# Both parts of split weights written by GpSimd's DMAs, in a two-layer decoder trunk

## The chip, the core and the metric

The kernel runs on one core of one Trainium2 chip. The metric is device time in microseconds of one execution: 842.21 us before the change, the median of 3 runs (840.75 to 844.86). The core has five engines that work side by side, each through its own queue of instructions: TensorE (PE; the loading of its weights is listed as PEld), VectorE (DVE), ScalarE (ACT), GpSimd (POOL) and SyncE (SP, which here only issues DMAs). DMAs are carried out by 16 transfer engines that all queues share.

## The reference, cut to what matters

Two layers over 520 rows: a prompt of 512 positions and 8 sample rows. Layer 0 is one wide input projection (1024 to 7 x 1024), a convolution of width 31 with a layer norm (A), a short gated convolution (B), and an output projection; layer 1 projects to u, v and a gate (3 x 2048), mixes v within chunks of 128 positions, and projects back. After each comes a layer norm of the residual sum.

```
z = einsum('bld,de->ble', x, w_in)                         # layer 0: a_val, a_gate, b_post, c_pre, h, g
a = silu(layer_norm(causal_dwconv(a_val * sigmoid(a_gate))))
bo = b_post * causal_dwconv(c_pre * h)
x = layer_norm(alpha * x + einsum('ble,ed->bld', concat(a, bo) * silu(g), w_out))
...
u, v, g = split(einsum('bld,de->ble', x, w_in_c))          # layer 1
y = gelu(u) * (tril(w_s) @ layer_norm(gelu(v)) + b_s) * silu(g)
x = layer_norm(alpha * x + einsum('ble,ed->bld', y, w_out_c))
```

Everything is float32.

## The kernel before

The channels lie on the 128 partitions, the 520 rows along the free dimension. All projection weights are cut into 136 **units**, each a tile of 128 x 1024 float32 (512 KB): 1024 input channels as 8 k tiles of 128, by 128 output channels. One unit gives 128 output channels for all rows.

TensorE multiplies in float32r, which keeps fewer bits than float32. So every operand is split into two float32r parts: hi, the value cast to float32r, and lo, the value less hi. A product is hi·hi + lo·hi + hi·lo, three matmuls for each k tile and half of the rows (`mm2`, L152 to L163): 8 x 2 x 3 = 48 matmuls of 260 columns per unit. Both parts of a unit are needed from its second matmul on.

The first two units come with the input rows and are split in pieces (L177 to L213). The other 134 go through `load_unit` (L116): SyncE issues the load into a raw tile (L119; three buffers), ScalarE casts it to hi (L121), and VectorE or GpSimd subtracts hi from raw to give lo (L124). GpSimd has units 4 to 45 and 66 to 83 (`ON_POOL`, L127), VectorE the rest. The hi and lo tiles come from 12 buffers (`W`), six units' worth; units 70, 71, 134 and 135 (`EXTRA`) lie in another pool. `unit(n)` (L132) hands out unit n and loads ahead to unit n + 5 (`LEAD`). So the tiles of unit n can be written once TensorE has finished unit n - 6.

The order of the instructions of each engine is set by a scheduler when the kernel is built, from the order of the code, priorities (`background` for the wide convolution, `soon` for some steps) and what each instruction waits for. On the chip each engine then follows that order strictly: an instruction that waits holds back all that stand behind it.

The stages in order of TensorE's work: units 0 to 31, in turns of gate, val, c and h (L283 to L339), while VectorE runs the wide convolution (`acc`, L269, 240 steps) and the short one (`sB`, L332, 16 steps); post (L388), gb (L406) and the first half of the output projection (`z_o`, L453); ga; the second half of the projection with the layer norm (`out_part`, L473); then layer 1: v (L622 to L643, units 72 to 87), u and gc with the mix (`c_group`, L728), the first half of the output projection (`z_q`), u and gc again, and `out_part` for the end. `out_part` goes through its eight units twice, once for each half of the rows, and ends with the norm.

On GpSimd there are, besides its subtractions, small copies of the 8 sample rows (L307, L326, L612, L725), the stores of the convolution caches, two loads (L588, L590) and some steps of the last layer norm (L537, L549).

Of the kernel before, what the change touches and what calls it, by code (L numbers as in the profile page):

```python
# [9 lines left out]
F32 = mybir.dt.float32  # L10
# [3 lines left out]
ALU = mybir.AluOpType  # L14
AX = mybir.AxisListType

P = 128
D = 1024
# [5 lines left out]
KT = 8  # L24
# [8 lines left out]

# columns of the packed per-channel parameters
PA_W = 0
# [15 lines left out]
def decoder_kernel(  # L51
# [19 lines left out]
    nc = tc.nc  # L71
# [3 lines left out]
    wpool = ctx.enter_context(tc.tile_pool(name="wpool", bufs=1))  # L75
# [35 lines left out]

# [1 line left out]
    n_units = 2 + wu.shape[0]  # L113
    units = [None, None]

    def load_unit(wtag=("W", 12)):  # L116
        n = len(units)
        raw = wpool.tile([P, KT, P], F32, tag="raw", name=f"raw_{n}", bufs=3)
        nc.sync.dma_start(raw, wu[n - 2])  # L119
        hi = wpool.tile([P, KT, P], F32R, tag=wtag[0], name=f"whi_{n}", bufs=wtag[1])  # L120
        nc.scalar.copy(hi, raw)  # L121
        lo = wpool.tile([P, KT, P], F32R, tag=wtag[0], name=f"wlo_{n}", bufs=wtag[1])
        eng = nc.gpsimd if n in ON_POOL else nc.vector
        eng.tensor_tensor(lo, raw, hi.bitcast(F32), op=ALU.subtract)  # L124
        units.append((hi, lo))

    ON_POOL = set(range(4, 46)) | set(range(66, 84))  # L127
    EXTRA = set()
# [35 lines left out]

    # products of a constant until the first rows are there, so that the array's clock is up by then
    warm = const.tile([P, P], BF16, name="warm")
# [4 lines left out]

    # the input rows come with the first two weight units, one k tile after the other, and the
    # products follow in that order
    xh, xl = [], []
# [4 lines left out]
    for k in range(KT):  # L179
# [7 lines left out]
        cuts = 2 if k == 0 else 1  # L187
# [29 lines left out]
    nc.sync.dma_start(pa, pa_in)  # L217
    # powers of two, so float32r holds them as well
    ones_r = const.tile([P, P], F32R, name="ones_r")
# [10 lines left out]

    # ================= layer 0 =================
    unit(1)
# [49 lines left out]
    n = 0  # L282
    for i in range(KT):  # L283
# [56 lines left out]

    # the sample rows of both convolutions
    nc.gpsimd.dma_start(cbs_out, xb)
# [5 lines left out]
        op=ALU.mult,  # L348
# [21 lines left out]

    # layer norm of the wide convolution over the channels, then silu
    def mean_of(m, src, name):
        """the sum of src / D over the channels, from its two float32r parts"""
        both = tpool.tile([P, T], F32R, tag="B", name=f"parts_{name}", bufs=4)
        nn = src.shape[-1]
        hi, lo = both[:, :nn], both[:, TH : TH + nn]
        nc.scalar.copy(hi, src)
        nc.vector.tensor_tensor(lo, src, hi.bitcast(F32), op=ALU.subtract)
        nc.tensor.matmul(m, ones_r, hi, start=True, stop=False)
        nc.tensor.matmul(m, ones_r, lo, start=False, stop=True)  # L380
# [13 lines left out]
    def split_y(i, g, other, tag, parts):  # L394
        """y = g * other as its two parts, in that many cuts of the rows"""
        h = y_slot(F32R, f"yh_{tag}{i}")
        lo = y_slot(F32R, f"yl_{tag}{i}")
        for j in range(parts):
            c = slice(j * T // parts, (j + 1) * T // parts)
            nc.vector.tensor_tensor(g[:, c], g[:, c], other[:, c], op=ALU.mult)  # L400
            nc.scalar.copy(h[:, c], g[:, c])
            nc.vector.tensor_tensor(lo[:, c], g[:, c], h[:, c].bitcast(F32), op=ALU.subtract)
        yh.append(h)
        yl.append(lo)
# [68 lines left out]
    def out_part(base, c0, c1, yh, yl, res, lnc, done, last=False, pool_sub=()):  # L473
        """The second half of an output projection for the rows c0..c1, the residual, and the layer
        norm over the channels. The sums of the norm are of the rows less the mean of their first
        512 channels, so that no large mean cancels in the variance."""
        c = slice(c0, c1)
# [107 lines left out]

    # ================= layer 1 =================
    wt = wpool.tile([P, NH, P], F32, tag="M", name="wt", bufs=4)
    nc.gpsimd.dma_start(wt, wsT_in)  # L588
    bs = wpool.tile([P, NH, P], F32, tag="M", name="bs", bufs=4)
    nc.gpsimd.dma_start(bs, bs_in)  # L590
    # wt[s, h, t] is kept where s <= t
    nc.gpsimd.affine_select(
        wt, wt, pattern=[[0, NH], [1, P]], compare_op=ALU.is_ge, fill=0.0, base=0, channel_multiplier=-1
    )
    # and its float32r parts, for the column sums
    wth, wtl = [], []
# [53 lines left out]
    def v_finish():  # L650
# [5 lines left out]
        for i in range(NV):  # L656
            for c in range(NC):
# [7 lines left out]
                )  # L665
        # column sums of the causal weights, for the shift of the norm
        for j in range(2):
# [5 lines left out]
            )  # L673
        # the sample rows' layer norm
        ssum = tiny.tile([P, NS], F32, name="ssum")
# [113 lines left out]
def _units(w, e0, e1):  # L789
    """[1024, e] columns e0..e1 as [n, 128 (k inside), 8 (k tile), 128]"""  # L790
    w = w[:, e0:e1]
    n = (e1 - e0) // P
    return w.reshape(KT, P, n, P).transpose(2, 1, 0, 3)


def _chan(a, n):
    """[..., n*128] -> [128, n, ...]"""
    a = a.reshape(a.shape[:-1] + (n, P))
    k = a.ndim
    return a.transpose((k - 1, k - 2) + tuple(range(k - 2)))  # L800
# [86 lines left out]
```

## Time and profile before

| | |
|---|---|
| Median of 3 runs | 842.21 us (840.75 to 844.86) |
| Span of the profiled execution, first to last instruction | 840.8 us |
| TensorE's granted clock, mean | 0.991 |
| ScalarE's casts L121 | 134, 1047 ns each |
| GpSimd's subtractions L124 | 60, 2434 ns each |
| VectorE's subtractions L124 | 74, 1222 ns each |
| Wide convolution L269 on VectorE | 240, 748 ns each |

The page of the profile gives no other time of its own execution than the span. In the rows that follow, a group of instructions reads: line, engine, operation, output<-inputs, shapes, count, then busy time in us and the mean of one in ns, then the idle time of the engine just before them and what ended it. Rows of DMA issues read: output<-input, issuing queue, count, KB each, median us from issue to landing. A row of waits reads: who waited <- whom for, us in total, times, the longest. In the chain of waits and the timeline a row starts with its start and its length in us. In a tile's own view the durations are the shortest, the median and the longest in ns.

The busy shares of the engines in 40 equal slices of the span (digits are tenths; 9 is 90% or more):

```
PE   9989999998999999999999999999999999999994
DVE  5899999999994487356696333495455433625566
ACT  5423322333124346333466533333432133333243
POOL 0844355544340000024252711101000000000022
DMA  8533333223223452424050522204223233222011
```

### The profile page before, as it was taken

How to read it: one execution, taken by the hardware profiler on the slowest of the kernel's cores; microseconds unless marked ns; L12 is line 12 of the kernel's file. 1: busy time of each engine (PE TensorE's matmuls, PEld its weight loads, DVE VectorE, ACT ScalarE, POOL GpSimd, SP SyncE). 2: the span in 40 equal slices, each digit the busy share in tenths (PEclk: the TensorE clock that was granted, in tenths of full speed). 3: DMA queues.
4: the chain of work that ended last, by engine and by line, in shares of the span. 5: the costliest groups of instructions: out<-in, count | busy, mean ns of one | idle time of the engine just before them, and what ended most of it. 6: DMA issues, size and time to landing. Idle time of an engine off the chain costs nothing.

```text
span 840.8 us, 15982 instructions
## 1 busy us (share of the span) xinstructions
PE 816.4 (97%) x6792; PEld 813.8 (97%) x6792; DVE 557.8 (66%) x894; ACT 309.5 (37%) x470; POOL 193.7 (23%) x178
## 2 busy tenths in 40 slices
PE   9989999998999999999999999999999999999994
PEld 8989999998999999999999999999999999999993
DVE  5899999999994487356696333495455433625566
ACT  5423322333124346333466533333432133333243
POOL 0844355544340000024252711101000000000022
PEclk9999999999999999999999999999999999999998
DMA  8533333223223452424050522204223233222011
GB/s 301 164 103 101 101 103 102 96 82 130 72 79 101 122 166 66 126 76 126 26 166 12 171 81 82 95 24 156 77 76 95 82 101 94 83 79 99 1 51 51
DMA packets 27110, 82.38 MB, mean 98 GB/s; under 512 B 3568, under 2 KB 7296, under 8 KB 27040
## 3 DMA queue, kind: packets, MB, share of 16 engines
q1 hardware_dynamic: 26000, 79.01, 30.1%
q0 software_dynamic: 1040, 2.36, 0.7%
q8 instruction: 53, 0.87, 0.4%
q14 instruction: 17, 0.14, 0.1%
HBM read 77.91 MB, written 3.44 MB: 97 GB/s over the span
## 4 chain that ended last, share of the span: by engine, by line
PE 71%; DVE 23%; DMA 2%; issue 2%; ACT 1%; SPq 0%; POOL 0%; ACTq 0%; DVEq 0%; POOLq 0%
DVE acc L269 14%; PE z_gc L157 11%; PE z_u L157 11%; PE z_p L141 9%; PE z_v L157 7%; PE z_q L157 5%; PE z_o L157 5%; PE z_gb L157 5%; PE z_ga L157 5%; PE z_post L157 4%; PE z_v L141 4%; DVE sB L332 3%; DMA raw<-in_wu 2%; PE mix L713 2%; PE vt L615 1%
## 5 line engine op out<-in xcount | busy, mean ns | idle before, releaser
L121 ACT CAST whi<-raw 128x1024 fp32r<-128x1024 f32 x134 | 140.0, 1047 | 300.6 <-issue 66.6
L124 POOL TENSOR_TENSOR wlo<-raw,whi 128x1024 fp32r<-128x1024 f32 x60 | 145.6, 2434 | 262.6 <-ACT whi L121 262.3
L124 DVE TENSOR_TENSOR wlo<-raw,whi 128x1024 fp32r<-128x1024 f32 x74 | 90.2, 1222 | 131.0 <-ACT whi L121 131.0
L269 DVE SCALAR_TENSOR_TENSOR acc<-apad,pa,acc 128x512 f32<-128x512 f32 x240 | 166.6, 748 | 2.5 <-ACT acc L266 0.8
L157 PE MATMUL z_gc<-x1h,whi 128*128 128x260 f32 x256 | 72.9, 285 | 0.0
L157 PE MATMUL z_u<-x1h,whi 128*128 128x260 f32 x256 | 72.4, 283 | 0.0
L157 PE MATMUL z_gc<-x1h,wlo 128*128 128x260 f32 x256 | 72.0, 281 | 0.0
L157 PE MATMUL z_u<-x1l,whi 128*128 128x260 f32 x256 | 72.0, 281 | 0.0
L157 PE MATMUL z_gc<-x1l,whi 128*128 128x260 f32 x256 | 72.0, 281 | 0.0
L157 PE MATMUL z_u<-x1h,wlo 128*128 128x260 f32 x256 | 72.0, 281 | 0.0
L157 PEld LDWEIGHTS z_u<-x1h,wlo 128*128 128x128 f32 x256 | 48.1, 188 | 0.1
L157 PEld LDWEIGHTS z_gc<-x1h,wlo 128*128 128x128 f32 x256 | 48.2, 188 | 0.0
L157 PEld LDWEIGHTS z_u<-x1h,whi 128*128 128x128 f32 x256 | 48.1, 188 | 0.1
L157 PEld LDWEIGHTS z_gc<-x1l,whi 128*128 128x128 f32 x256 | 48.1, 188 | 0.0
L157 PEld LDWEIGHTS z_u<-x1l,whi 128*128 128x128 f32 x256 | 48.1, 188 | 0.0
L157 PEld LDWEIGHTS z_gc<-x1h,whi 128*128 128x128 f32 x256 | 48.1, 188 | 0.0
L725 POOL COPY mix<-mixs 128x8 f32<-128x8 f32 x16 | 3.5, 226 | 186.5 <-DVE gu L752 174.1
L157 PE MATMUL z_v<-x1h,whi 128*128 128x260 f32 x160 | 46.0, 287 | 0.0
L157 PE MATMUL z_v<-x1h,wlo 128*128 128x260 f32 x160 | 45.0, 281 | 0.0
L157 PE MATMUL z_v<-x1l,whi 128*128 128x260 f32 x160 | 44.9, 281 | 0.0
L157 PE MATMUL z_post<-xh,whi 128*128 128x260 f32 x128 | 36.8, 288 | 4.2 <-DVE sB L392 4.2
L157 PE MATMUL z_h<-xh,whi 128*128 128x260 f32 x128 | 36.9, 288 | 4.0 <-DVE apad L306 4.0
(259 smaller groups left out, 2758.5 us busy)
## 6 DMA issues: line engine op xcount, KB each, us to landing
raw<-in_wu SPq DMA_DIRECT2D x134, 512.0 KB, 3.6
xr<-in_xT SPq DMA_DIRECT2D x8, 260.0 KB, 4.6
x<-in_xT SPq DMA_DIRECT2D x7, 260.0 KB, 4.4
out_y<-r SPq DMA_DIRECT2D x8, 130.0 KB, 1.8
out_y<-out SPq DMA_DIRECT2D x4, 260.0 KB, 2.2
raw_s<-in_w SPq DMA_DIRECT2D x8, 128.0 KB, 4.2
xs<-in_cache_a SPq DMA_DIRECT2D x2, 496.0 KB, 9.2
out_cas<-xs POOLq DMA_DIRECT2D x2, 496.0 KB, 4.5
```

The costliest lines, as they stand in the source:

```text
L121: nc.scalar.copy(hi, raw)
L124: eng.tensor_tensor(lo, raw, hi.bitcast(F32), op=ALU.subtract)
L141: nc.tensor.matmul(ps, a[:, k, :], b[k][:, c], start=(k == 0 and j == 0), stop=(k == KT - 1 and j == 2),)
L157: nc.tensor.matmul(z[h][:, :TH], a[:, k, :], b[k][:, hs(h)], start=(k == 0 and j == 0), stop=(k == KT - 1 and j == 2),)
L269: nc.vector.scalar_tensor_tensor(acc[i], apads[i][:, j : j + SEQ], pa[:, i, PA_W + j : PA_W + j + 1], acc[i], op0=ALU.mult, op1=ALU.add,)
L332: nc.vector.scalar_tensor_tensor(s[:, :SEQ], ch[:, j : j + SEQ], pa[:, i, PB_W + j : PB_W + j + 1], s[:, :SEQ], op0=ALU.mult, op1=ALU.add,)
L615: nc.tensor.transpose(m[:, c * P : (c + 1) * P], vt[i][:, c * P : (c + 1) * P], ident)
L713: nc.tensor.matmul(m[:, c * P : (c + 1) * P], vtok[i][:, c * P : (c + 1) * P], wt[:, h, :], start=True, stop=True)
L725: nc.gpsimd.tensor_copy(t[:, SEQ:], mixs[:, i, :])
```

## The change

The raw tile goes, and with it the choice between VectorE and GpSimd. GpSimd issues a DMA that reads the weights as float32 and writes them as float32r into hi, casting on the way. ScalarE writes -hi into lo. GpSimd then issues a second DMA that reads the same weights again and adds them to lo in place, so that lo holds the weights less hi. Each unit is so read twice from memory, and the low part crosses ScalarE before its second DMA may start. The units, their buffers, the lead and all else stay as they were.

```diff
     def load_unit(wtag=("W", 12)):
         n = len(units)
-        raw = wpool.tile([P, KT, P], F32, tag="raw", name=f"raw_{n}", bufs=3)
-        nc.sync.dma_start(raw, wu[n - 2])
         hi = wpool.tile([P, KT, P], F32R, tag=wtag[0], name=f"whi_{n}", bufs=wtag[1])
-        nc.scalar.copy(hi, raw)
+        nc.gpsimd.dma_start(hi, wu[n - 2])
         lo = wpool.tile([P, KT, P], F32R, tag=wtag[0], name=f"wlo_{n}", bufs=wtag[1])
-        eng = nc.gpsimd if n in ON_POOL else nc.vector
-        eng.tensor_tensor(lo, raw, hi.bitcast(F32), op=ALU.subtract)
+
+        nc.scalar.mul(lo, hi.bitcast(F32), -1.0)
+        nc.gpsimd.dma_start(lo, wu[n - 2], accum_op=ALU.add)
         units.append((hi, lo))
 
-    ON_POOL = set(range(4, 46)) | set(range(66, 84))
     EXTRA = set()
```

The rest of the diff takes comments out. Lines of the changed kernel stand two lower than before: the DMAs are L119 and L123, the negation is L122.

The scheduler orders GpSimd's queue anew. Three places show how. In the rows a name is followed by the unit's number (or that of another tile) and a buffer number: `whi_86_5688` is the high part of unit 86.

GpSimd at the start of layer 0, behind its first memsets, before the change (it waits for the first gate tile, then subtracts for units 4 and on):

```order
L324 MEMSET ch_7_2403 128x2
L307 COPY xs_0_335<-apad_0_347 128x8
L308 DMA out_cap<-apad_0_347 128x30
L124 TENSOR_TENSOR wlo_4_321<-raw_4_317,whi_4_319 128x1024
L124 TENSOR_TENSOR wlo_5_327<-raw_5_323,whi_5_325 128x1024
```

The same place after the change:

```order
L322 MEMSET ch_7_2368 128x2
L119 DMA whi_2_290<-in_wu 128x1024
L119 DMA whi_3_310<-in_wu 128x1024
L123 DMA wlo_2_292<-in_wu 128x1024
L305 COPY xs_0_330<-apad_0_342 128x8
L306 DMA out_cap<-apad_0_342 128x30
L119 DMA whi_4_315<-in_wu 128x1024
L123 DMA wlo_3_312<-in_wu 128x1024
L119 DMA whi_5_320<-in_wu 128x1024
L123 DMA wlo_4_317<-in_wu 128x1024
```

The loads of units 2 and 3 stand ahead of everything that waits for a product; the low part of unit 3 and all later loads stand behind the copy out of the first gate tile (`apad`). Each low-part DMA stands two DMAs behind its high part.

GpSimd during the post stage of layer 0, where it prepares units 41 to 45 of the gb stage, before: subtractions alone, one after the other.

```order
L124 TENSOR_TENSOR wlo_41_2672<-raw_41_2668,whi_41_2670 128x1024
L124 TENSOR_TENSOR wlo_42_2728<-raw_42_2724,whi_42_2726 128x1024
L124 TENSOR_TENSOR wlo_43_2784<-raw_43_2780,whi_43_2782 128x1024
L124 TENSOR_TENSOR wlo_44_2840<-raw_44_2836,whi_44_2838 128x1024
L124 TENSOR_TENSOR wlo_45_2896<-raw_45_2892,whi_45_2894 128x1024
```

The same units after:

```order
L119 DMA whi_41_2629<-in_wu 128x1024
L119 DMA whi_42_2684<-in_wu 128x1024
L123 DMA wlo_41_2631<-in_wu 128x1024
L123 DMA wlo_42_2686<-in_wu 128x1024
L119 DMA whi_43_2739<-in_wu 128x1024
L123 DMA wlo_43_2741<-in_wu 128x1024
L119 DMA whi_44_2794<-in_wu 128x1024
L119 DMA whi_45_2849<-in_wu 128x1024
L123 DMA wlo_44_2796<-in_wu 128x1024
L123 DMA wlo_45_2851<-in_wu 128x1024
```

Units 41 and 42 go as a pair, two high parts and then two low parts, so that one DMA stands between the two of a unit; unit 43 goes alone, its low part directly behind its high part; then a pair again.

GpSimd in the v stage, from unit 83 on, before: VectorE has the subtractions from unit 84 on, and only the small copies of the sample rows are left.

```order
L124 TENSOR_TENSOR wlo_82_5314<-raw_82_5310,whi_82_5312 128x1024
L612 COPY vs_5142<-v_5_5340 128x8
L124 TENSOR_TENSOR wlo_83_5569<-raw_83_5565,whi_83_5567 128x1024
L612 COPY vs_5142<-v_6_5619 128x8
L612 COPY vs_5142<-v_7_5688 128x8
```

The same stage after:

```order
L119 DMA whi_86_5688<-in_wu 128x1024
L610 COPY vs_5067<-v_8_5673 128x8
L123 DMA wlo_86_5690<-in_wu 128x1024
L119 DMA whi_87_5756<-in_wu 128x1024
L610 COPY vs_5067<-v_9_5741 128x8
L123 DMA wlo_87_5758<-in_wu 128x1024
```

Every unit's low part stands directly behind its own high part, with one small copy between, and the next unit's high part behind that. Counted over GpSimd's whole queue, with the copies and stores left aside: of the 134 low-part DMAs 47 stand directly behind their own high-part DMA, 62 have one other weight DMA between, and 25 have two or more.

## The prediction

> **What bounds the kernel now.** I read the shares of the engines first, then the idle time of TensorE, then the table of DMA issues.
>
> ```profile
> span 840.8 us, 15982 instructions
> PE 816.4 (97%) x6792; PEld 813.8 (97%) x6792; DVE 557.8 (66%) x894; ACT 309.5 (37%) x470; POOL 193.7 (23%) x178
> ```
>
> TensorE is busy for 816.4 of 840.8 us. It works through 136 weight units, so one unit takes it 816.4/136 = 6.0 us, with everything else that it does spread over them. The chain of waits shows the same pace in the v stage, one unit of 48 products each 6.17 us:
>
> ```profile
> 491.22 5.73 PE z_v L157 x48
> 497.39 5.74 PE z_v L157 x48
> ```
>
> Only 24.4 us of the span are not TensorE work. Of TensorE's own waits two matter, and both end at VectorE in the first 212 us:
>
> ```profile
> PE z_post L157 <- DVE sB L392: 4.2, 1, 4.2
> PE z_h L157 <- DVE apad L306: 4.0, 1, 4.0
> ```
>
> The rest of the idle time lies at the start and behind the last products, at the end. No change to the weights' way in can therefore gain much more than 4.2 + 4.0 = 8.2 us. It can lose far more: each unit needs both of its parts, so if a unit takes longer than 6.0 us to come in, all 134 units that are loaded in this way pay the difference. What they cost now:
>
> ```profile
> raw<-in_wu SPq DMA_DIRECT2D x134, 512.0 KB, 3.6
> xs<-in_cache_a SPq DMA_DIRECT2D x2, 496.0 KB, 9.2
> out_cas<-xs POOLq DMA_DIRECT2D x2, 496.0 KB, 4.5
> wt<-in_wsT POOLq DMA_DIRECT2D x1, 512.0 KB, 5.9
> ...
> q1 hardware_dynamic: 26000, 79.01, 30.1%
> ```
>
> One load per unit, issued from SyncE, lands 3.6 us after its issue. On the transfer engines, 30.1% of 840.8 us for 79.01 MB is 312 GB/s, so a unit of 0.524 MB holds them 1.7 us. SyncE has nothing else to do, and its loads wait for a free raw buffer, not for each other:
>
> ```profile
> SPq L119 <- DVE wlo L124: 357.1, 67, 22.0
> SPq L119 <- POOL wlo L124: 264.3, 52, 24.4
> ```
>
> So now the supply has slack: transfer, cast and subtraction stand on four different engines and run side by side for different units.
>
> **What the change removes.** The cast on ScalarE becomes a negation on ScalarE of the same size, so nothing changes there. The subtractions go, 74 on VectorE and 60 on GpSimd:
>
> ```profile
> L124 DVE TENSOR_TENSOR wlo<-raw,whi 128x1024 fp32r<-128x1024 f32 x74 | 90.2, 1222 | 131.0 <-ACT whi L121 131.0
> L124 POOL TENSOR_TENSOR wlo<-raw,whi 128x1024 fp32r<-128x1024 f32 x60 | 145.6, 2434 | 262.6 <-ACT whi L121 262.3
> L121 ACT CAST whi<-raw 128x1024 fp32r<-128x1024 f32 x134 | 140.0, 1047 | 300.6 <-issue 66.6
> ```
>
> Most of that lies beside TensorE's products and is worth nothing. In layer 0 there is more to it, because VectorE is full there and its convolution work runs into GpSimd's:
>
> ```profile
> 36.37 7.68 DVE L332 SCALAR_TENSOR_TENSOR sB<-ch,pa,sB 128x512 f32<-128x512 f32 x1
> ...
> 36.37 7.13 POOL L124 TENSOR_TENSOR wlo<-raw,whi 128x1024 fp32r<-128x1024 f32 x3
> ...
> L332 DVE SCALAR_TENSOR_TENSOR sB<-ch,pa,sB x16: 739/1154/7678, 33.4 to 207.1; 128x512 f32<-128x512 f32 x16
> ...
> L332 DVE SCALAR_TENSOR_TENSOR sB<-ch,pa,sB 128x512 f32<-128x512 f32 x16 | 29.3, 1831 | 0.9 <-ACT sB L330 0.9
> ```
>
> One sB step, 0.74 us at its fastest, lasted 7.68 us, exactly while three subtractions ran on GpSimd. Sixteen steps took 29.3 us in place of 16 x 0.74 = 11.8. With GpSimd's subtractions gone, about 17.5 us of VectorE time in layer 0 come free, which is more than the 8.2 us of TensorE's two waits: these two can vanish.
> The Trainium skill, "SBUF — State Buffer", section "Who interferes with whom", has this rule: a VectorE instruction with two SBUF inputs and a GpSimd instruction that reads SBUF exclude each other. The trace agrees (7.68 us beside 7.13 us).
>
> **What the change adds.** Two transfers per unit in place of one, both from GpSimd's queue, with ScalarE's negation between them. Per unit the chain is: issue of the casting load, its landing, the negation, issue of the accumulating load, its landing. The prices:
>
> ```profile
> L588 POOL DMA_DIRECT2D wt<-in_wsT x1: 568/568/568, 436.0 to 436.0; - x1
> L121 ACT CAST whi<-raw x134: 1030/1047/1055, 15.8 to 779.1; 128x1024 fp32r<-128x1024 f32 x134
> ...
> DMA to landing us min/median/max: 3.3/3.6/8.4
> ```
>
> - Issue on GpSimd: 0.57 us. Negation: 1.05 us, by the cast of the same tile. Together 1.62 us.
> - Landing L of the casting load. No casting load is in the trace. The same bytes as a plain load from this queue took 5.9 us (wt), a store of nearly the size 4.5 us; I take the middle, 5.2. Bounds: 3.6 us (SyncE's loads) and 9.2 us (the slowest such row, xs).
> - Time a that the accumulating load holds the transfer engines. It is not in the trace either. It reads the weights and the tile it adds to: as much as one read, 1.7 us, or two, 3.4. I take 3.4, since twice the bytes go in; the upper bound is twice that, 6.8, if arithmetic halves the rate.
>
> How much of the chain overlaps is decided by the order in which GpSimd issues. It is one queue: a low-part load that waits for its negation holds back all that stand behind it, the next high-part load first, and the small copies of GpSimd too. Of the 134 low-part loads, 47 stand directly behind their own high-part load, 62 have one other weight load between, 25 have more. I let transfers of this one queue be served in order.
>
> - Directly behind: the next high-part load is issued when the low-part load has been, and its data come behind that load's. Cycle = a + L + 1.62 = 3.4 + 5.2 + 1.62 = 10.2 us a unit.
> - One between, mostly two high parts and then two low parts: two accumulating transfers, one landing, 1.62 us; the second high part lands while the first is negated. (2a + L + 1.62)/2 = (6.8 + 5.2 + 1.62)/2 = 6.8 us a unit.
> - More between: a + 1.7 = 5.1 us, hidden under TensorE's 6.0, so 6.0.
>
> Supply: 47 x 10.2 + 62 x 6.8 + 25 x 6.0 = 479 + 422 + 150 = 1051 us. That replaces 134 x 6.0 = 804 us of products. The five units loaded ahead are a stock that is used up once; of their 5 x 6.0 = 30 us the chain itself (issue to landed low part, about 10 us) takes a third, so they are worth at most 20 us, which I leave out here. The 8.2 us that VectorE gives back are worth nothing while TensorE waits for weights: where that stall goes, the weights are late next.
>
> What else stands behind the new waits. On GpSimd the small copies do, such as the sample rows of a mix tile:
>
> ```profile
> L725 POOL COPY mix<-mixs 128x8 f32<-128x8 f32 x16 | 3.5, 226 | 186.5 <-DVE gu L752 174.1 <-DVE gu L400 10.8 <-DVE mixs L701 1.5
> ```
>
> VectorE's product of the layer's output waits for that copy and TensorE's output projection for the product. A copy can come late by one cycle, 10.2 us, no more than the weights of the same stage are late, so I add nothing; with weights in time it would cost up to 4.2 us (10.2 - 6.0) per group of four. On ScalarE a negation that waits for its casting load holds back the emptying of a z tile. There are two of them, so TensorE has one unit, 6.0 us, before it notices; in the forecast it is waiting for weights anyway.
>
> Around the supply: GpSimd is free at about 2.5 us; the first loads meet the input rows, where the worst load landed 8.4 us after its issue in place of 3.6, so 4.8 more. After the last unit there follow its first-half products (24 x 0.12 = 2.9 us), and the second half of the rows with the final norm:
>
> ```profile
> 808.15 10.78 PE z_p L141 x90
> ...
> 826.93 0.44 PE mean L517 x2
> ```
>
> Eight units of 24 products at 0.12 us end at 826.93, so they begin near 826.9 - 23 = 803.9, 36.9 us before the span ends. Sum: 2.5 + 4.8 + 1051 + 2.9 + 36.9 = 1098 us of span. The profiled span of 840.8 is 1.4 us under the median of the runs shown (842.21); with that, **1100 us**.
>
> With the low bounds (L = 3.6, a = 1.7): 47 x 6.9 and the rest hidden under 6.0, so 47 x 0.9 = 42 us more than now, less the 20 us of lead and with the start, some 865. With L = 4.5 and a = 1.7 the 47 cost 7.8 each, 85 us more, so near 905. With the high bounds (9.2 and 6.8): 47 x 17.6 + 62 x 12.2 + 25 x 8.5 = 1796, about 1840.
>
> **Rules of the skill against it.** The Trainium skill, "DMA: Bandwidth & Descriptors", section "Anatomy of one DMA — SWDGE (gpsimd) path", gives about 2.0 us plus bytes/436 GB/s for such a DMA: 3.2 us for a unit, an estimate from that page. By that L, and with a = 1.7, the 47 cost 6.5 each and the sum would be near 850, the lower end of rival 1; the wt row, 5.9 us, speaks against it.
> The Trainium skill, "SBUF — State Buffer", section "🔬 SBUF: two separate sides", says that GpSimd cannot write descriptors while VectorE runs in a two-port mode. What this could cost here is one block:
>
> ```profile
> 546.84 16.52 DVE L658 TENSOR_SCALAR vtok<-vtok,mv,rs 128x128 f32<-128x128 f32 x64 [0.41 <-POOL rs L655]
> ```
>
> If weight loads stand still through it, up to 16.5 us are added to the sum; by the trace alone, none. Only GpSimd's own issues in this block of the changed profile can tell.
>
> **The rivals.**
> 1. *The transfers cost no more than plain ones* (a = 1.7, L = 3.6 to 4.5). For it: the queue moved plain bytes no slower than SyncE's. The 47 units still cost 6.9 to 7.8 us against 6.0: 850 to 930 us.
> 2. *The cast and the addition themselves are slow*, so the transfer engines saturate and the order no longer matters: with L = 9.2 and a = 6.8, 1400 to 1840 us. For it: each element has to go through arithmetic; no row here shows the rate.
> 3. *Not slower than before*: the supply stays under 6.0 us a unit and VectorE's relief remains. This needs a + L + 1.62 under 6.0 for the 47, so with a = 1.7 an L under 2.7 us, less than any 512 KB row here; from that point on, the 8.2 us are won, against 5 or so at the start: 833 to 845 us. A negation and a landing that overlap better than I count would do the same.
>
> That the change does not do what it says is excluded: all 134 units go this way in the order.
>
> **How the numbers follow.** Forecast (930 to 1400 us): 0.56. Rival 1: 0.18. Rival 2: 0.19. Rival 3: 0.07. The predicted time is the forecast's, 1100. The range runs from 870, which leaves out rival 3 and a third of rival 1 (0.13), to 1650, which leaves out the upper third of rival 2 (0.07). About 0.5% is what a measurement of this kernel can tell from no change: 838 to 846.4 us. Faster by more has half of rival 3, 0.03; within it the other half, 0.04; slower the rest, 0.93.
>
> **What would show it.** In the changed profile TensorE's share falls to near 75%, its waits name the low part, and they are longest where GpSimd's order is high, low, high, low (the v stage and most of layer 1). The table of DMA issues gives L and the accumulating load's landing; the queues' share of 16 engines shows whether a is 1.7, 3.4 or more. sB steps near 0.74 us would confirm VectorE's relief. I am wrong if TensorE keeps 6.0 us a unit in the v stage (rivals 1 or 3), or if the transfer engines are near full all through (rival 2).

## The result and the profile after

| | before | after |
|---|---|---|
| Median on the same chip | 842.57 us (840.75 to 844.86, 4 runs) | 985.64 us (979.49 to 985.79, 4 runs) |
| Span of the profiled execution | 840.8 us | 984.1 us |
| TensorE's granted clock, mean | 0.991 | 0.943 |

The ratio is 1.168, 95% interval [1.165, 1.172]: the changed kernel is 17% slower. The forecast was 1100 us, with a range of 870 to 1650.

The page of the changed kernel, shares of the engines and DMA queues:

```profile
span 984.1 us, 16079 instructions
PE 862.9 (88%) x6792; PEld 851.4 (87%) x6792; DVE 435.7 (44%) x820; ACT 307.4 (31%) x470; POOL 234.4 (24%) x386
q0 software_dynamic: 39632, 142.89, 63.3%
q1 hardware_dynamic: 6704, 8.74, 2.7%
```

No resource is full. The transfer engines are at 63.3 + 2.7 = 66%, VectorE has lost 122 us of work, and TensorE's idle time has gone from 24.4 to 984.1 - 862.9 = 121.2 us. The next view, the groups of instructions, says where the waiting is (busy time and mean ns, then idle time before them and what ended most of it); under it two rows of DMA issues with the median time to landing:

```profile
L122 ACT ACTIVATE wlo<-whi 128x1024 fp32r<-128x1024 f32 x134 | 141.8, 1058 | 546.4 <-DMA whi<-in_wu 518.4
L123 POOL DMA_DIRECT2D wlo<-in_wu x134 | 117.3, 877 | 632.3 <-ACT wlo L122 591.6
...
whi<-in_wu POOLq DMA_DIRECT2D x134, 512.0 KB, 6.6
wlo<-in_wu POOLq DMA_DIRECT2D x134, 512.0 KB, 5.7
```

ScalarE stands 518.4 us in front of a negation whose casting load has not landed, and GpSimd 591.6 us in front of an accumulating load whose negation is not done. Two engines that are busy for a quarter to a third of the span are blocked for over half of it. The timeline of the v stage shows one turn of this chain. First GpSimd's rows (start, length, instruction, and in brackets the idle time before it and what ended it), then ScalarE's, then TensorE's one wait:

```profile
598.22 0.86 POOL L123 DMA_DIRECT2D wlo<-in_wu  x1 [6.91 <-ACT wlo L122]
598.76 0.88 POOL L119 DMA_DIRECT2D whi<-in_wu  x1
...
606.81 0.86 POOL L123 DMA_DIRECT2D wlo<-in_wu  x1 [6.97 <-ACT wlo L122]
```

```profile
596.87 1.06 ACT L122 ACTIVATE wlo<-whi 128x1024 fp32r<-128x1024 f32 x1 [6.51 <-DMA whi<-in_wu]
597.83 0.59 ACT L639 ACTIVATE v<-z_v 128x520 f32<-128x520 f32 x1
...
605.45 1.06 ACT L122 ACTIVATE wlo<-whi 128x1024 fp32r<-128x1024 f32 x1 [6.56 <-DMA whi<-in_wu]
```

```profile
598.47 0.66 PE L613 MATMUL vt<-ident,v 128*128 128x128 f32 x4 [2.15 <-ACT v L639]
```

The low part is issued at 598.22, the next high part 0.54 us later; its data are there and the negation starts 6.69 us after that (605.45), the negation takes 1.06, and 0.30 us later, at 606.81, the next low part goes out. The turn closes without TensorE: 0.54 + 6.69 + 1.06 + 0.30 = 8.59 us a unit, against the 6.0 us that TensorE needs. TensorE notices it in a place where no weights are named: it waits 2.15 us for `v`, since ScalarE, which copies the products out, does so only at 597.83, behind the negation that began at 596.87, for a unit that is needed much later. The waits of TensorE, largest first (us, times, longest), say the same; of the waits for weights the largest is the last row:

```profile
PE z_u L155 <- ACT gu L734: 16.5, 3, 8.7
PE z_gate L155 <- ACT c L315: 14.9, 3, 5.9
PE vt L613 <- ACT v L639: 13.9, 9, 3.2
...
PE z_c L155 <- DMA wlo<-in_wu: 1.8, 1, 1.8
```

### The profile page after: what moved, and what is told of

Read it like the earlier page. It is cut to its first block, busy times and chain, and to the rows that moved or that the text cites. A ratio compares the mean times of both kernels' runs of the same rounds, so it can differ in the third digit from the quotient of the medians.

```text
span 984.1 us, 16079 instructions
## 1 busy us (share of the span) xinstructions
PE 862.9 (88%) x6792; PEld 851.4 (87%) x6792; DVE 435.7 (44%) x820; ACT 307.4 (31%) x470; POOL 234.4 (24%) x386
## 3 DMA queue, kind: packets, MB, share of 16 engines
q0 software_dynamic: 39632, 142.89, 63.3%
HBM read 148.17 MB, written 3.44 MB: 154 GB/s over the span
## 4 chain that ended last, share of the span: by engine, by line
issue 52%; POOL 15%; DMA 14%; PE 13%; ACT 3%; DVE 2%; POOLq 0%; SPq 0%; ACTq 0%; DVEq 0%
DMA whi<-in_wu 14%; POOL wlo L123 7%; POOL whi L119 6%; PE z_p L139 4%; PE z_gc L155 2%; PE z_u L155 2%; PE z_v L139 2%; ACT wlo L122 1%; PE z_first L205 1%; DMA x<-in_xT 1%; DVE acc L267 1%; POOL mix L723 0%; PE mix L711 0%; POOL xb L324 0%; POOL out_cbp L325 0%
## 5 line engine op out<-in xcount | busy, mean ns | idle before, releaser
L122 ACT ACTIVATE wlo<-whi 128x1024 fp32r<-128x1024 f32 x134 | 141.8, 1058 | 546.4 <-DMA whi<-in_wu 518.4
L123 POOL DMA_DIRECT2D wlo<-in_wu x134 | 117.3, 877 | 632.3 <-ACT wlo L122 591.6
L119 POOL DMA_DIRECT2D whi<-in_wu x134 | 105.9, 815 | 63.8 <-PE z_p L139 19.7
L155 PE MATMUL z_u<-x1h,whi 128*128 128x260 f32 x256 | 77.3, 302 | 16.5 <-ACT gu L734 16.5
L750 DVE TENSOR_TENSOR gu<-silu_c,gu 128x520 f32<-128x520 f32 x16 | 11.2, 700 | 157.0 <-ACT silu_c L749 157.0
L155 PEld LDWEIGHTS z_u<-x1h,whi 128*128 128x128 f32 x256 | 52.8, 206 | 17.2 <-ACT gu L734 17.2
L617 DVE BATCH_NORM_STATS2 stats<-vtok 128x6 f32<-128x128 f32 x64 | 14.0, 280 | 98.7 <-ACT vtok L615 98.7
L155 PEld LDWEIGHTS z_u<-x1h,wlo 128*128 128x128 f32 x256 | 52.9, 207 | 0.1
L155 PEld LDWEIGHTS z_u<-x1l,whi 128*128 128x128 f32 x256 | 52.6, 206 | 0.1
L155 PE MATMUL z_gate<-xh,whi 128*128 128x260 f32 x112 | 34.7, 310 | 14.9 <-ACT c L315 14.9
```

What stands on the lines that cost most here:

```text
L119: nc.gpsimd.dma_start(hi, wu[n - 2])
L122: nc.scalar.mul(lo, hi.bitcast(F32), -1.0)
L123: nc.gpsimd.dma_start(lo, wu[n - 2], accum_op=ALU.add)
L155: nc.tensor.matmul(z[h][:, :TH], a[:, k, :], b[k][:, hs(h)], start=(k == 0 and j == 0), stop=(k == KT - 1 and j == 2),)
L617: nc.vector.bn_stats(stats[:, c, i, :], t[:, c * P : (c + 1) * P])
L750: nc.vector.tensor_tensor(t, g, t, op=ALU.mult)
```

## The experiments

The theories put to the test: **theory 1**, order: a low part that stands directly behind its own high part in GpSimd's queue holds everything back for a landing and a negation. **Theory 2**, the transfer engines: two transfers, one with an addition, are too much for them. **Theory 3**, GpSimd's time to issue. **Theory 4**, ScalarE: TensorE waits because the negation blocks ScalarE. **Theory 5**, the five units loaded ahead are too small a stock. All ratios are to the kernel before on the same chip.

| run | median us | ratio to before, 95% | TensorE's clock |
|---|---|---|---|
| changed kernel | 985.64 | 1.168 [1.165, 1.172] | 0.943 |
| e_hi_ahead | 842.66 | 1.000 [0.999, 1.001] | 0.991 |
| e_lead4 | 983.02 | 1.166 [1.163, 1.169] | 0.939 |
| e_stock | 850.97 | 1.010 [1.008, 1.012] | 0.988 |
| e_no_chain | 837.37 | 0.996 [0.994, 0.997] | 0.990 |
| e_two_casts | 840.36 | 0.998 [0.997, 0.999] | 0.989 |
| e_acc_alone | 838.31 | 0.996 [0.994, 0.997] | 0.991 |
| e_cast_alone | 923.35 | 1.097 [1.095, 1.100] | 0.975 |
| e_neg_dve | 986.35 | 1.173 [1.169, 1.177] | 0.937 |
| e_neg_twice | 873.87 | 1.039 [1.035, 1.043] | 0.978 |
| e_best | 827.79 | 0.983 [0.981, 0.985] | 0.994 |
| e_best_cast | 833.05 | 0.989 [0.987, 0.991] | 0.994 |

**Only the order.** In e_hi_ahead each high part is loaded one unit before its low part, within the same 12 buffers, and so 4 units ahead in place of 5; e_lead4 is its control, the lead of 4 alone. The diff is cut (`...`); `AHEAD` is 1.

```diff
-LEAD = 5
+LEAD = 4
...
-        hi = wpool.tile([P, KT, P], F32R, tag=wtag[0], name=f"whi_{n}", bufs=wtag[1])
-        nc.gpsimd.dma_start(hi, wu[n - 2])
+        def high(m):
...
+            nc.gpsimd.dma_start(hi, wu[m - 2])
+            ready[m] = hi
+
+        for m in range(n, min(n + 1 + AHEAD, n_units)):
+            if m not in ready:
+                high(m)
+        hi = ready[n]
```

> 12 weight buffers as in the changed kernel, units loaded 4 ahead in place of 5, and each high part loaded one unit before its low part in the program (112 low-part loads with two weight loads between). Theory 1 (order): 840 to 865 us with no more memory. Theories 2 and 3 (transfer engines, issue time): 970 to 1000 us. Theory 5 (too small a stock): slower than the changed kernel, above 990 us, since one unit less is ahead.

> Only the lead goes from 5 units to 4; GpSimd's order of loads stays that of the changed kernel (47 directly behind, 62 with one between). The control for the kernel with the high part ahead. Theory 1 (order, where a stock is used up once): 985 to 1000 us. Theory 5 (the stock carries the supply): well above, 1010 us or more. Theory 4 (TensorE waits since ScalarE stands behind a negation that waits for its load, not for weights): ScalarE meets the negation as late as before, 985 us within 10.

Measured: 842.66 us and 983.02 us. (In GpSimd's order 112 low parts have four weight loads between themselves and their high part, not two as the expectation says: the casting loads of the next two units and the accumulating loads of the two before.) This distance takes off 140 us; the lead of 4 alone takes off at most a few (983.02 is 2 us under what theory 1 had for it, and the range of its runs, 980.09 to 990.51, overlaps that of the changed kernel). The page of e_hi_ahead, its DMA queue, and the same piece of GpSimd's timeline in the v stage:

```profile
span 839.6 us, 16108 instructions
...
q0 software_dynamic: 39632, 142.89, 77.2%
```

```profile
501.79 0.55 POOL L125 DMA_DIRECT2D whi<-in_wu  x1 [4.17 <-PE z_v L166]
502.75 0.86 POOL L134 DMA_DIRECT2D wlo<-in_wu  x1 [0.41 <-ACT wlo L133]
...
507.95 0.55 POOL L125 DMA_DIRECT2D whi<-in_wu  x1 [4.15 <-PE z_v L166]
508.92 0.85 POOL L134 DMA_DIRECT2D wlo<-in_wu  x1 [0.42 <-ACT wlo L133]
```

GpSimd now waits 4.17 us for TensorE, that is for a free buffer, and only 0.41 us for ScalarE; a turn takes 507.95 - 501.79 = 6.16 us, TensorE's own pace. The same 142.89 MB keep the transfer engines at 77.2% with no loss, so at 63.3% they were not what held the changed kernel: theory 2 falls, and theory 3 with it. Theory 5 falls by e_lead4.

**More buffers, same code.** e_stock has one W buffer more. What that does is not to lengthen the lead: the scheduler now puts two loads, the low part of the unit before and the high part of the unit behind, between a high part and its low part.

```diff
-    def load_unit(wtag=("W", 12)):
+    def load_unit(wtag=("W", 13)):
...
-            raw = wpool.tile([P, 4, 2, P], F32, tag="raw", name=f"raw_s{k}", bufs=3)
+            raw = wpool.tile([P, 4, 2, P], F32, tag="raw", name=f"raw_s{k}", bufs=2)
```

> 13 weight buffers in place of 12 (the raw buffers of the start go from 3 to 2 for it). The loads and the negations stay; but in GpSimd's order 123 low-part loads now have a high-part load of the next unit between themselves and their own high part, where in the changed kernel 47 had none. Theory 1 (the order makes the loss: casting load, negation and accumulating load run one after the other in one queue): every unit hides its landing, so 840 to 865 us. Theory 2 (the transfer engines are the limit, 768 KB of extra reads and writes per unit): the same bytes move, so 970 to 990 us. Theory 3 (GpSimd's 1.7 us of issue per unit): 970 to 990 us.

Measured: 850.97 us. 135 us go with one weight buffer more and one raw buffer less. Two weight loads between seem not quite enough where e_hi_ahead has four: TensorE's idle time is 850.6 - 818.6 = 32.0 us against 839.6 - 816.1 = 23.5, and e_stock still has waits for ScalarE (4.2 us for `sg`, 1.8 for `v`, 1.6 for `c`) of which e_hi_ahead has none over 0.5. (The 768 KB of the expectation stand in no trace: what the core read from HBM grew from 77.91 to 148.17 MB, 0.52 MB a unit.)

**Only the wait.** e_no_chain keeps both loads, has an even worse order than the changed kernel (120 low parts directly behind, not 47), and takes away what the negation waits for; e_two_casts has no negation and no addition.

```diff
-        nc.scalar.mul(lo, hi.bitcast(F32), -1.0)
+        nc.scalar.mul(lo, warm[:, None, :].to_broadcast([P, KT, P]), -1.0)
         nc.gpsimd.dma_start(lo, wu[n - 2], accum_op=ALU.add)
```

```diff
-        nc.scalar.mul(lo, hi.bitcast(F32), -1.0)
-        nc.gpsimd.dma_start(lo, wu[n - 2], accum_op=ALU.add)
+        nc.gpsimd.dma_start(lo, wu[n - 2])
```

> Left out: the negated high part. ScalarE writes a constant into the low part in its place, from a tile that is always there, so the low part is the weights less one and the output is not the reference's. Both loads, their kinds, their bytes and the issue on GpSimd stay, and 120 of 134 low parts stand directly behind their own high part; only the wait of the negation for the casting load's landing is gone. Theory 1 (the chain landing, negation, issue): 835 to 865 us. Theory 2 (transfer engines) and theory 3 (issue time): 970 to 990 us.

> Left out: the negation and the addition; a second casting load writes the weights into the low part, so the output is not the reference's. Two DMAs of GpSimd's queue per unit, neither with a wait for the other. Theory 1: 833 to 850 us, and TensorE's waits for VectorE gone. Theory 3 (issue time): 970 us or more. Beside the kernel without the wait it prices the accumulation itself: by theory 1 no difference over 10 us, by theory 2 some 100 us.

Measured: 837.37 and 840.36 us. With an order no better than it was, 148 us go when the low part no longer depends on its high part's landing; with the dependence as it was, 143 us go when the order lets it land (e_hi_ahead). It takes both to lose the time, and theory 1 says just that. The addition itself costs no time here. What it costs the transfer engines comes out of e_two_casts, where all 268 loads of units cast:

```profile
whi<-in_wu POOLq DMA_DIRECT2D x134, 512.0 KB, 4.0
wlo<-in_wu POOLq DMA_DIRECT2D x134, 512.0 KB, 4.8
...
q0 software_dynamic: 39632, 142.89, 53.5%
```

53.5% of 839.1 us (its span) is 449 us for 268 loads: c = 1.68 us each. In the changed kernel 63.3% of 984.1 is 623 us for 134 pairs, 4.65 each, so a = 4.65 - 1.68 = 2.97 us for an accumulating load. The next run, e_acc_alone, gives it more directly, since its GpSimd issues no other load of units:

```profile
q0 software_dynamic: 20336, 72.62, 51.3%
```

51.3% of 836.6 us is 429 us for 134, 3.2 each. So a is about 3 us.

**Each half alone.** e_acc_alone brings the high part by SyncE and a cast on ScalarE, e_cast_alone the low part by a subtraction on VectorE or GpSimd as before the change.

```diff
+        raw = wpool.tile([P, KT, P], F32, tag="raw", name=f"raw_{n}", bufs=3)
+        nc.sync.dma_start(raw, wu[n - 2])
...
-        nc.gpsimd.dma_start(hi, wu[n - 2])
+        nc.scalar.copy(hi, raw)
```

```diff
+        raw = wpool.tile([P, KT, P], F32, tag="raw", name=f"raw_{n}", bufs=3)
+        nc.sync.dma_start(raw, wu[n - 2])
...
-        nc.scalar.mul(lo, hi.bitcast(F32), -1.0)
-        nc.gpsimd.dma_start(lo, wu[n - 2], accum_op=ALU.add)
+        eng = nc.gpsimd if n in ON_POOL else nc.vector
+        eng.tensor_tensor(lo, raw, hi.bitcast(F32), op=ALU.subtract)
```

> The casting load is undone: raw comes from SyncE, ScalarE casts it to the high part and negates that, and GpSimd's accumulating load remains. No low-part load has a landing ahead of it in GpSimd's queue. Theory 1: 832 to 845 us; the subtractions are still gone, so TensorE's two waits for VectorE (8.2 us) go. Theory 2: the same bytes plus none saved, 970 us or more. Theory 4 with ScalarE as the limit: 2.1 us of ScalarE per unit, busy about 450 of 840 us, and raw lands without GpSimd, so no more than 845 us.

> The accumulating load is undone: the casting load from GpSimd writes the high part, raw comes from SyncE and the subtraction stands on VectorE and GpSimd as before the change; ScalarE neither casts nor negates. Theory 1: no wait of GpSimd's queue for a negation, but 60 subtractions on GpSimd wait for their casting load and hold back the next load: 838 to 870 us, TensorE's waits for VectorE in layer 0 as before the change. Theory 2: 940 us or more. Theory 4 (only a waiting negation on ScalarE hurts): 838 to 845 us.

Measured: 838.31 us, as expected, and 923.35 us, a miss: 53 us above the upper end that theory 1 was given. GpSimd's timeline of e_cast_alone in layer 0, and the largest of TensorE's waits:

```profile
83.41 2.40 POOL L124 TENSOR_TENSOR wlo<-raw,whi 128x1024 fp32r<-128x1024 f32 x1 [3.92 <-issue]
85.76 0.56 POOL L121 DMA_DIRECT2D whi<-in_wu  x1
90.69 2.41 POOL L124 TENSOR_TENSOR wlo<-raw,whi 128x1024 fp32r<-128x1024 f32 x1 [4.37 <-issue]
93.03 0.57 POOL L121 DMA_DIRECT2D whi<-in_wu  x1
...
98.05 2.36 POOL L124 TENSOR_TENSOR wlo<-raw,whi 128x1024 fp32r<-128x1024 f32 x1 [3.76 <-issue]
```

```profile
PE z_post L158 <- POOL wlo L124: 11.1, 7, 2.3
```

It is the same fault with another instruction: a subtraction of 2.4 us stands on GpSimd directly behind the load that it needs, the next load behind it, and a turn takes 98.05 - 90.69 = 7.36 us. Units 4 to 45, whose subtractions stand on GpSimd, take 7.74 us a turn in the mean (from 28.46 to 345.94 us, 41 turns), and 42 x 1.74 = 73 us is what they cost: TensorE starts the ga stage at 412.6 us, before the change at 340.1, so 72.5 later. The other 18 add only 6.5 us by the start of the v stage (551.4 in place of 472.4), and nothing within it. Together that is 79 of the 81 us measured (923.35 - 842.25, the kernel before of those runs). The timeline names no release for these waits ("issue"); that they are waits for the landing follows from the times, since from the load's issue to the subtraction it takes 90.69 - 85.76 = 4.93 us, and the median landing of this kernel's casting loads is this row:

```profile
whi<-in_wu POOLq DMA_DIRECT2D x134, 512.0 KB, 5.0
```

Here little of the consumer's own work stands behind the waiting instruction, and so TensorE's waits do name the weights.

**Who negates.** e_neg_dve moves the negation to VectorE; e_neg_twice makes it longer.

```diff
-        nc.scalar.mul(lo, hi.bitcast(F32), -1.0)
+        nc.vector.tensor_scalar_mul(lo, hi.bitcast(F32), -1.0)
```

```diff
-        nc.scalar.mul(lo, hi.bitcast(F32), -1.0)
+        nc.scalar.copy(lo, hi.bitcast(F32))
+        nc.scalar.mul(lo, lo.bitcast(F32), -1.0)
```

> The negation goes from ScalarE to VectorE; GpSimd's order of loads stays nearly as it is (46 directly behind, 52 with one between). Theory 1 alone (the chain sets the pace, whoever negates): 970 to 1000 us, and VectorE waits for the casting load where ScalarE did. Theory 4 (the loss comes about because ScalarE, which empties the z tiles, stands behind a negation that waits): TensorE no longer waits for ScalarE; the pace is then the supply's own, some 900 to 940 us, with waits that name the low part.

> ScalarE does the negation in two passes, a copy and then a negation in place: 1.06 us more per unit on ScalarE and in the chain between the two loads. In GpSimd's order of this kernel 94 low-part loads have two weight loads between themselves and their own high part, 27 have one, and one has none (changed kernel: 47 with none, 62 with one). If the length of the chain alone set the time, it would be slower than the changed kernel, 985 + 134 x 1.06 = 1127 us at most. Theory 1 (where the loads stand in the order decides): 845 to 880 us in spite of the longer chain. Theory 4 (ScalarE's time): slower than 985 us.

Measured: 986.35 us, no other time than with ScalarE, and 873.87 us, faster by 112 us with 134 x 1.06 = 142 us more work on ScalarE. TensorE's largest waits in e_neg_dve:

```profile
PE vs_mean L676 <- DVE ssum L674: 12.8, 1, 12.8
PE mix L711 <- DVE mix L715: 12.2, 3, 5.2
PE vs_var L686 <- DVE qsum L684: 8.2, 1, 8.2
PE z_q L155 <- DVE yl_c L400: 7.9, 3, 4.4
```

The waits have moved from ScalarE to VectorE and the time has stayed, so ScalarE's time is not the cause. That the time is the same to 1 us is partly chance: VectorE's negation takes 0.70 us, and the turns of the 46 units directly behind 8.2 us in place of 9.0, but two negations stand on VectorE behind the 16.5 us block of `vtok`, and one low part follows the one before only after 21.9 us. Nor does e_neg_dve alone exclude theory 4 in a wider form, since VectorE, too, works for TensorE. e_cast_alone does: no negation is there to block ScalarE, and yet 81 us go, where theory 4 had 838 to 845 us. Whichever engine waits passes the delay on, but the pace comes from GpSimd's chain. e_neg_twice says the same from the other side: a longer chain in a better order beats a shorter one in a worse order.

**A version that beats both.** TensorE's largest waits in e_acc_alone lie at the start, where the loads meet the input rows:

```profile
PE z_c L156 <- DMA wlo<-in_wu: 5.1, 1, 5.1
PE z_h L156 <- ACT sg L290: 3.4, 1, 3.4
```

To take these away, e_best subtracts the first six units on VectorE (its diff is shown against e_acc_alone). e_best_cast brings the first six in by SyncE's load, ScalarE's cast and VectorE's subtraction, and goes on as e_hi_ahead.

```diff
         nc.scalar.copy(hi, raw)
...
-        nc.scalar.mul(lo, hi.bitcast(F32), -1.0)
-        nc.gpsimd.dma_start(lo, wu[n - 2], accum_op=ALU.add)
+        if n < 8:
+            nc.vector.tensor_tensor(lo, raw, hi.bitcast(F32), op=ALU.subtract)
+        else:
+            nc.scalar.mul(lo, hi.bitcast(F32), -1.0)
+            nc.gpsimd.dma_start(lo, wu[n - 2], accum_op=ALU.add)
```

> Raw from SyncE, cast on ScalarE; the low part of the first six loaded units is subtracted on VectorE as before the change, that of all others comes by negation and accumulating load. The kernel with the accumulating load alone lost 5.1 us at about 20 us of the span to a late low part, while the start's transfers filled the engines, and 3.4 us to ScalarE; both should go here. 829 to 835 us, faster than the kernel before by 0.9 to 1.5%.

> As the kernel with the high part one unit ahead (both loads on GpSimd), but the first six loaded units come as before the change: raw from SyncE, cast on ScalarE, subtraction on VectorE. The kernel with the high part ahead lost its 5 to 6 us at the start, where TensorE waited for the input rows' parts behind twelve weight loads from GpSimd. 831 to 838 us; if the casting load costs something of its own, above the kernel with raw from SyncE by that much.

Measured: 827.79 and 833.05 us. The first is 1.7% faster than the kernel before, 1.2 us better than its expectation. (In front of the waits that e_best_cast was to remove, GpSimd had issued three weight loads in e_hi_ahead, from 2.40 to 4.24 us, not twelve as its expectation says.) The page of e_best, and all of TensorE's waits of 0.2 us or more:

```profile
span 825.9 us, 16146 instructions
PE 812.2 (98%) x6792; PEld 810.6 (98%) x6792; DVE 435.6 (53%) x826; ACT 432.5 (52%) x598; POOL 154.8 (19%) x246
```

```profile
PE warm L172 <- DVE warm L169: 1.1, 1, 1.1
PE z_p L143 <- DMA wlo<-in_wu: 0.5, 1, 0.5
PE z_c L159 <- DVE wlo L124: 0.2, 1, 0.2
```

TensorE's two waits for VectorE are gone and nothing has come in their place. The spans of the two versions differ by 831.3 - 825.9 = 5.4 us. TensorE's busy time is 813.4 - 812.2 = 1.2 us of it, and most of the rest are waits that e_best lacks: at the entry into layer 1 2.1 us for `x1h` and 1.5 for a low part, and 0.7 for the first input rows.

## Why the prediction was right, and where it was not

**Right: the mechanism.** The prediction saw that GpSimd's single queue puts landing, negation and issue one behind the other, that this makes 10.2 us a unit where nothing lies between, and that 134 units pay for it. e_no_chain and e_hi_ahead, which each remove one half of that condition, give the whole loss back. The sign that was to show it wrong, 6.0 us a unit in the v stage, did not come: the turn there is 8.59. Rival 2 is excluded (the transfer engines at 66% here, and fuller in e_hi_ahead without loss), rival 3 did not come. Of rival 1 the short landing came true, not the cheap accumulation.

**Mis-sized: the landing L, and a little of a.** The cycle a + L + 1.62 was put at 3.4 + 5.2 + 1.62 = 10.2 us; the v stage shows 8.59. The chain's own work was right (0.54 + 1.06 + 0.30 = 1.90 for 1.62). What failed is a + L: 6.69 us measured for 8.6. With a = 2.97 that leaves L = 3.7 us for 5.2, with a = 3.2 3.5 us; this L is a difference, not a row. I had taken the middle of two rows of GpSimd's queue (5.9 and 4.5 us); the row of SyncE's loads, 3.6, which I held as the low bound, was the nearest, and e_two_casts agrees roughly (median 4.0 us, shortest 3.6). For the casting load's own time on the transfer engines, c, 1.7 us was right (1.68).

How this adds up against the sum, by the accumulating loads' row (shortest, median and longest in ns, first and last start):

```profile
L123 POOL DMA_DIRECT2D wlo<-in_wu x134: 846/873/1207, 17.9 to 930.3; - x134
```

From the first to the last of the 134, 133 turns, it takes 930.3 - 17.9 = 912.4 us, where the prediction had 1051. With each of these loads put to its place in GpSimd's order, the 47 directly behind their high part took 422 us, 9.0 each (8.1 to 10.9, median 8.65), in place of 479; those with one load between 381, in place of 422; the other 25 took 110, in place of 150 (together 912, rounded). The 381 us hold two turns of 23.1 and 27.6 us on the way into layer 1, in which GpSimd's next casting load waited 16.9 and 15.9 us for TensorE to free a buffer; the prediction has no such wait. Without these two, a unit with one load between took 5.6 us, and the prediction's own (2a + L + 1.62)/2 gives 5.6 with a = 2.97 and L = 3.7. The start and the end took 984.1 - 912.4 = 71.7 us in place of 47.1: the first low part is issued at 17.9 us, not at 2.5 + 4.8 = 7.3, and 53.8 us, not 2.9 + 36.9 = 39.8, follow the last. So 139 us too much in the supply, 25 too little around it: 1098 - 139 + 25 = 984. That the forecast came this near is in part luck: its prices were too high, and the two long turns and the start and end that it left out or cut short made up some of that.

**Wrong: how TensorE feels it.** The text said that TensorE's waits would name the low part. They name ScalarE, with 1.8 us at most for a weight. I had let one z tile cover a late negation and took TensorE to be waiting for weights anyway. But a negation stands in ScalarE's queue for a unit that is some five ahead, in front of the copy that TensorE needs now. So in the v stage the stock was not drawn down first and then missed. The low part that goes out at 598.22 is that of unit 89, by GpSimd's order; it lands at 603.6, and TensorE first reads it at 625.1. While TensorE waits for `v` up to 598.47, both parts of its next three units, 86 to 88, have landed. The blocked engine stops its consumer while weights lie ready. (The stock does run down elsewhere: TensorE's three waits for a low part lie at the start and on the way into layer 1.) That e_lead4 costs nothing, and that the waits follow the negation to VectorE, bears this out; it changes the place of the waits, not the pace.

**Right and worth nothing: VectorE's relief.** The sixteen sB steps, shortest, median and longest in ns:

```profile
L330 DVE SCALAR_TENSOR_TENSOR sB<-ch,pa,sB x16: 742/746/753, 43.1 to 240.3; 128x512 f32<-128x512 f32 x16
```

All sixteen take 0.75 us, none the 7.68 of before. In the versions whose supply keeps up, this relief shows: e_acc_alone, e_no_chain and e_best are faster than before.

**Too low: the most that could be gained.** The prediction held that no change to the weights' way in can gain much more than 8.2 us. e_best gains 840.8 - 825.9 = 14.9 us of span. TensorE's idle time falls by 24.4 - 13.7 = 10.7 us, the two waits and some of 0.6 to 0.8 us, and its busy time by 816.4 - 812.2 = 4.2. Before the change the granted clock is 0.50 from 51.1 to 54.5 and from 211.6 to 214.9 us, right behind the two waits; in e_best it is 1.00 from 20 to 785 us.

**TensorE's share** is 88%, not 75%. A shorter span gives 816.4/984.1 = 83% of it; the rest is slower products, below.

**The two rules that were weighed.** By the Trainium skill, "SBUF — State Buffer", section "🔬 SBUF: two separate sides", GpSimd cannot write descriptors while VectorE runs in a two-port mode. That left open a standstill of GpSimd's issues while VectorE works through `vtok`. In the changed kernel this block lies from 638.1 to 654.2 us, and within it GpSimd issued:

```profile
L656 DVE TENSOR_SCALAR vtok<-vtok,mv,rs x64: 332/338/406, 638.1 to 654.2; 128x128 f32<-128x128 f32 x64
...
641.52 0.93 POOL L123 DMA_DIRECT2D wlo<-in_wu  x1 [3.50 <-ACT wlo L122]
642.20 0.83 POOL L119 DMA_DIRECT2D whi<-in_wu  x1
650.93 0.97 POOL L123 DMA_DIRECT2D wlo<-in_wu  x1 [7.91 <-ACT wlo L122]
651.50 0.96 POOL L119 DMA_DIRECT2D whi<-in_wu  x1
```

Four issues of 0.83 to 0.97 us, each on the release of the chain: no standstill, at most 0.1 us each above the usual 0.86 to 0.88. The one whole turn within the block, 641.52 to 650.93, took 9.41 us, inside the 8.1 to 10.9 of the other units directly behind, so a slowing of less than 1 us can't be told. Whether VectorE was in the mode that the rule speaks of, no run shows. By the Trainium skill, "DMA: Bandwidth & Descriptors", section "Anatomy of one DMA — SWDGE (gpsimd) path", a unit would land in 3.2 us, an estimate from that page. A median of 4.0 was measured in e_two_casts and about 3.7 follows for the changed kernel, nearer to that estimate than to my 5.2.

## What to carry to other kernels

So it was in this kernel: when one in-order queue issues a transfer and, right behind it, something that needs its result, every unit pays the whole landing; the length of the chain and the load on the transfer engines matter less than how many other issues stand between the two. Put the dependent step one unit later in the code, or give the pool the one buffer that lets a scheduler do so, before judging a new way of loading. And look at what stands behind a helper instruction on its engine: one that waits for a prefetch blocks the consumer's own work there, however full the stock is, and the consumer's waits then name that work and not the prefetch.

## What was not expected of the hardware

**The clock behind a wait.** TensorE's granted clock fell to 0.943 in the mean, and its busy time grew by 862.9 - 816.4 = 46.5 us for the same 6792 products. Stretches of one turn in the v stage, right behind the wait that ended at 598.47 (busy time of PE, PEld, DVE, ACT, POOL with counts, then the clock, the DMA share, GB/s):

```profile
598.50:599.50 1.00, 1.00 (x9) 1.00 (x10) 0.58 (x3) 0.39 (x1) 1.00 (x3) 0.97 0.00 0
599.50:602.50 3.00, 3.00 (x16) 3.00 (x16) 0.29 (x2) 0.00 (x0) 0.34 (x2) 0.50 0.94 153
602.50:603.50 1.00, 1.00 (x9) 1.00 (x9) 0.00 (x0) 0.00 (x0) 0.00 (x0) 0.82 1.00 307
603.50:606.00 2.50, 2.50 (x23) 2.50 (x22) 0.00 (x0) 0.55 (x1) 0.00 (x0) 1.00 0.31 113
```

A wait of 2.15 us was followed, 1 us after it ended, by some 3.4 us at half of full speed (in the row of 3.00 us TensorE starts 16 products, 5.3 a us; at full speed, in the last row, 23 in 2.50, 9.2 a us), then full speed again. Not every such wait is: the one of 2.57 us a turn before ended at 589.93, and the clock was 1.00 from there to 597.93. In e_cast_alone, where most waits were 2.3 us or less, the mean clock stayed at 0.975. I read the slower products as filling idle time that the chain leaves (the turn of 8.59 us closes without TensorE); no run tested this.

**Prices of the two kinds of load.** A casting load of 512 KB held the transfer engines for 1.68 us, an accumulating one for about 3 us (2.97 or 3.2, by two workings), nearly twice as long, and yet e_no_chain, with one accumulating load a unit, needs no longer (837.37 us) than e_two_casts, with none (840.36 us).
